# An expert-combine kernel on one core: a third tile loaded in two pieces from two queues, and a first tile made token by token

## The chip, the core and the metric

The kernel runs on one core of one Trainium2 chip. The metric is the device time of that core in microseconds (us), as the median of several executions. The profile is of one execution. It names engines by short names: DVE is VectorE, ACT is ScalarE, SP is SyncE, POOL is GpSimd. "ACTq" and "SPq" are the instruction sequencers of ScalarE and SyncE, which issue DMA transfers. TensorE is not used.

## The reference: what is computed

Each of 16 x 1024 = 16,384 tokens has the outputs of two experts, 512 fp32 values each, and two weights. The result is their weighted sum.

```python
# expert_outputs: (16, 1024, 2, 512) fp32   combine_weights: (16, 1024, 2) fp32
weights = combine_weights[..., np.newaxis]
return np.sum(expert_outputs * weights, axis=2)      # (16, 1024, 512) fp32
```

The profile counts 67.24 MB read and 33.55 MB written, with three floating-point operations for each value of the result. Nothing is used twice.

## The kernel before

The 16,384 tokens lie over 128 partitions, 128 tokens in each: 120 in ten tiles of 12 tokens, and 8 in a last, smaller tile. Below, the tiles are numbered 0 to 10. A token is 2 x 512 fp32 = 4 KB in a partition, so a tile of 12 tokens is 48 KB in a partition and 6 MB in all, and its result 24 KB and 3 MB.

```python
J, LAST = 12, 8                       # tokens of a tile, of the last tile
wpool = ...tile_pool(name="w", bufs=1)
ipool = ...tile_pool(name="in", bufs=4)          # four input tiles
wt = wpool.tile([P, per * k], dt)                # all weights
for t, c in ((0, main), (main, LAST)):           # weights: two loads, ScalarE's queue
    nc.scalar.dma_start(out=wt[...], in_=cw(t, c))
# ... a first activation on a constant ("warm") ...
for g in range(last + 1):                        # last = 10
    et = ipool.tile([P, J, k * h], dt)
    ot = ...                                     # the result lies in the first half of et
    for a, m in ((0, 2), (2, c - 2)) if g == 0 else ((0, c),):     # loads, SyncE's queue
        nc.sync.dma_start(out=et[:, a : a + m], in_=eo(t0 + a, m), ...)
    if g < last - 1:                             # tiles 0 to 8: all on VectorE
        nc.vector.tensor_tensor(out=ek, in0=ek, in1=wb, op=mult)              # L78
        nc.vector.tensor_tensor(out=ot, in0=et[:, :, 0:h],
                                in1=et[:, :, h : 2 * h], op=add)              # L79
        nc.scalar.dma_start(out=o(t0, c), in_=ot)                             # L80
        continue
    for i in range(c):                           # tiles 9 and 10: first half on ScalarE
        nc.scalar.activation(out=et[:, i, 0:h], in_=et[:, i, 0:h], func=copy,
                             scale=wt[:, 2 * t : 2 * t + 1])                  # L86
        if g == last:                            # tile 10: token by token
            nc.vector.scalar_tensor_tensor(out=ot[:, i, :], in0=et[:, i, h : 2 * h],
                scalar=wt[...], in1=et[:, i, 0:h], op0=mult, op1=add)         # L90
    if g < last:                                 # tile 9: second half in one go
        nc.vector.tensor_tensor(out=x1, in0=x1, in1=w1..., op=mult)           # L101
        nc.vector.tensor_tensor(out=ot, in0=et[:, :, 0:h], in1=x1, op=add)    # L102
    nc.sync.dma_start(out=o(t0, c), in_=ot[:, 0:c])                           # L103
```

The result is written over the tile's own input, so a load of tile g+4 can only be issued when the store of tile g has landed. The framework decides the order of instructions on each engine.

Of the kernel before, what the change touches and what calls it, by code (L numbers as in the profile page):

```python
# [1 line left out]

# [4 lines left out]


@with_exitstack
def kernel(  # L10
    ctx: ExitStack,
    tc: tile.TileContext,
    expert_outputs: bass.AP,
    combine_weights: bass.AP,
    out: bass.AP,
):

    nc = tc.nc  # L20
    b, s, k, h = expert_outputs.shape
    assert k == 2
    n = b * s
    P = nc.NUM_PARTITIONS
    per = n // P
    assert per * P == n
    J, LAST = 12, 8
    main = per - LAST
    assert main % J == 0
    eo = expert_outputs.rearrange("b s k h -> (b s) (k h)")  # L30
    cw = combine_weights.rearrange("b s k -> (b s) k")
    o = out.rearrange("b s h -> (b s) h")

    def rows(x):

        a = x[0 : P * main, :].rearrange("(p t) f -> p t f", p=P)
        b = x[P * main : n, :].rearrange("(p t) f -> p t f", p=P)
        return lambda t, c: a[:, t : t + c, :] if t < main else b[:, t - main : t - main + c, :]

    eo, cw, o = rows(eo), rows(cw), rows(o)  # L40

    dt = mybir.dt.float32
    mult = mybir.AluOpType.mult
    add = mybir.AluOpType.add
    copy = mybir.ActivationFunctionType.Copy

    last = main // J

    wpool = ctx.enter_context(tc.tile_pool(name="w", bufs=1))
    ipool = ctx.enter_context(tc.tile_pool(name="in", bufs=4))  # L50

    wt = wpool.tile([P, per * k], dt)

    for t, c in ((0, main), (main, LAST)):
        nc.scalar.dma_start(
            out=wt[:, k * t : k * (t + c)].rearrange("p (t k) -> p t k", k=k), in_=cw(t, c)
        )

    warm = wpool.tile([P, 1], dt)
    nc.scalar.activation(out=warm, in_=nc.const_aps.tensor(1.0, (P, 1), dt), func=copy)  # L60

    for g in range(last + 1):
        et = ipool.tile([P, J, k * h], dt)

        ot = et.rearrange("p j f -> p (j f)")[:, 0 : J * h].rearrange("p (j f) -> p j f", f=h)
        t0, c = g * J, J if g < last else LAST

        for a, m in ((0, 2), (2, c - 2)) if g == 0 else ((0, c),):
            nc.sync.dma_start(  # L69
                out=et[:, a : a + m],  # L70
                in_=eo(t0 + a, m),
                max_dma_last_dim=k * h * 4 if g + a == 0 else None,
            )
        if g < last - 1:

            wb = wt[:, g * J * k : (g + 1) * J * k].unsqueeze(2).to_broadcast([P, J * k, h])
            ek = et.rearrange("p j (k h) -> p (j k) h", k=k)
            nc.vector.tensor_tensor(out=ek, in0=ek, in1=wb, op=mult)  # L78
            nc.vector.tensor_tensor(out=ot, in0=et[:, :, 0:h], in1=et[:, :, h : 2 * h], op=add)  # L79
            nc.scalar.dma_start(out=o(t0, c), in_=ot)  # L80
            continue


        for i in range(c):
            t = t0 + i
            nc.scalar.activation(  # L86
                out=et[:, i, 0:h], in_=et[:, i, 0:h], func=copy, scale=wt[:, 2 * t : 2 * t + 1]
            )
            if g == last:
                nc.vector.scalar_tensor_tensor(  # L90
                    out=ot[:, i, :],
                    in0=et[:, i, h : 2 * h],
                    scalar=wt[:, 2 * t + 1 : 2 * t + 2],
                    in1=et[:, i, 0:h],
                    op0=mult,
                    op1=add,
                )
        if g < last:
            w1 = wt.rearrange("p (t k) -> p t k", k=k)[:, t0 : t0 + c, 1:2]
            x1 = et[:, :, h : 2 * h]  # L100
            nc.vector.tensor_tensor(out=x1, in0=x1, in1=w1.to_broadcast([P, c, h]), op=mult)  # L101
            nc.vector.tensor_tensor(out=ot, in0=et[:, :, 0:h], in1=x1, op=add)  # L102
        nc.sync.dma_start(out=o(t0, c), in_=ot[:, 0:c])  # L103


# [1 line left out]
_INS = ['expert_outputs', 'combine_weights']  # L107
_OUTS = [((16, 1024, 512), 'float32')]


# [23 lines left out]
```

## Time and profile before

| what | value |
|---|---|
| time, median of 3 (lowest to highest) | 238.96 us (238.95 to 240.68) |
| span of the profiled execution | 237.3 us |
| VectorE busy | 193.9 us, 82% |
| ScalarE busy | 14.0 us, 6% |
| DMA packets, bytes, mean rate | 3728, 100.80 MB, 425 GB/s |
| a 6 MB load, from issue to landing (median) | 29.9 us |
| a 3 MB store from ScalarE, from issue to landing (median) | 32.7 us |
| multiply of a tile (L78), sum of a tile (L79) | 12.955 us, 6.558 us |
| one token on ScalarE (L86), on VectorE (L90) | 0.707 us, 0.748 us |

The busy share of an engine over the whole span is an average. Here two rows of the page matter together: the row of VectorE and the row of the DMA engines, each with one digit for a fortieth of the span. The time from issue to landing of a transfer includes the time in which it waits behind others in its queue.

### The profile page before, as it was taken

The numbers are of one execution on the slowest core, as the hardware profiler recorded it, in microseconds if no ns is written. First come the engines' busy times: TensorE is split into PE (matmuls) and PEld (weight loads), VectorE is DVE, ScalarE is ACT, GpSimd is POOL, SyncE is SP. The second block draws the span as 40 slices with busy tenths as digits, with TensorE's granted clock in tenths as the row PEclk, the third lists the DMA queues.
The fourth block names the chain that finished last, engine by engine and source line by source line (L and its number), as shares of the span: only waits on it lengthen the run. The fifth ranks groups of instructions, "written<-read, shape, count | busy, mean of one in ns | idle before, by whom it ended". The sixth has DMA issues, their size and how long they took to land.

```text
span 237.3 us, 154 instructions
## 1 busy us (share of the span) xinstructions
DVE 193.9 (82%) x28; ACT 14.0 (6%) x22; POOL 0.2 (0%) x4
## 2 busy tenths in 40 slices
DVE  0008999999999999999999879969996998785710
ACT  2000000000000000000000000000000000740800
POOL 0000000000000000000000000000000000000000
DMA  8999999989899999999897999999997979999997
GB/s 308 443 456 406 398 431 497 398 356 505 356 439 435 427 464 464 398 398 522 348 522 344 452 427 435 464 464 398 398 522 340 530 336 460 458 403 442 402 438 309
DMA packets 3728, 100.80 MB, mean 425 GB/s; under 512 B 528, under 2 KB 656, under 8 KB 912
## 3 DMA queue, kind: packets, MB, share of 16 engines
q1 hardware_dynamic: 2144, 72.35, 71.1%
q10 hardware_dynamic: 1584, 28.44, 27.9%
HBM read 67.24 MB, written 33.55 MB: 425 GB/s over the span
## 4 chain that ended last, share of the span: by engine, by line
DMA 59%; DVE 33%; ACT 2%; DVEq 0%; ACTq 0%; issue 0%; SPq 0%
DMA et<-in_expert_outputs_dram 30%; DMA out_dram<-et 29%; DVE et L78 22%; DVE et L79 11%; ACT et L86 2%; DVE et L90 1%; DVEq L129 0%; ACTq L129 0%; SPq L69 0%; DVEq L78 0%; ACTq L86 0%
## 5 line engine op out<-in xcount | busy, mean ns | idle before, releaser
L78 DVE TENSOR_TENSOR et<-et,wt 128x12288 f32<-128x12288 f32 x9 | 116.6, 12955 | 25.2 <-DMA et<-in_expert_outputs_dram 25.2
L79 DVE TENSOR_TENSOR et<-et 128x6144 f32<-128x6144 f32 x9 | 59.0, 6558 | 0.3
L86 ACT ACTIVATE et<-et,wt 128x512 f32<-128x512 f32 x20 | 12.5, 707 | 209.2 <-DMA et<-in_expert_outputs_dram 209.2
L90 DVE SCALAR_TENSOR_TENSOR et<-et,wt 128x512 f32<-128x512 f32 x8 | 5.6, 748 | 3.9 <-ACT et L86 3.7
L101 DVE TENSOR_TENSOR et<-et,wt 128x6144 f32<-128x6144 f32 x1 | 6.6, 6559 | 2.3 <-DMA et<-in_expert_outputs_dram 2.3
L102 DVE TENSOR_TENSOR et<-et 128x6144 f32<-128x6144 f32 x1 | 6.6, 6559 | 0.9 <-ACT et L86 0.9
L60 ACT ACT_TABLE_LOAD x1 | 1.3, 1283 | 1.7 <-issue 1.7
L60 ACT ACTIVATE warm<-const-float32-1.0 128x1 f32<-128x1 f32 x1 | 0.2, 202 | 0.0
L118 POOL MEMSET const-bfloat16-1.0<- 128x1 bf16 x1 | 0.1, 102 | 0.0
L118 POOL MEMSET const-uint8-127<- 128x1 uint8 x1 | 0.1, 102 | 0.0
L118 POOL MEMSET const-float32-0.0<- 128x1 f32 x1 | 0.1, 99 | 0.2 <-issue 0.2
L118 POOL MEMSET const-float32-1.0<- 128x1 f32 x1 | 0.1, 99 | 0.0
## 6 DMA issues: line engine op xcount, KB each, us to landing
et<-in_expert_outputs_dram SPq DMA_DIRECT2D x9, 6144.0 KB, 29.9
out_dram<-et ACTq DMA_DIRECT2D x9, 3072.0 KB, 32.7
et<-in_expert_outputs_dram SPq DMA_DIRECT2D x1, 5120.0 KB, 17.3
et<-in_expert_outputs_dram SPq DMA_DIRECT2D x1, 4096.0 KB, 25.1
out_dram<-et SPq DMA_DIRECT2D x1, 3072.0 KB, 14.6
out_dram<-et SPq DMA_DIRECT2D x1, 2048.0 KB, 10.0
et<-in_expert_outputs_dram SPq DMA_DIRECT2D x1, 1024.0 KB, 5.4
wt<-in_combine_weights_dram ACTq DMA_DIRECT2D x1, 120.0 KB, 4.4
```

The source lines that it names most:

```text
L60: nc.scalar.activation(out=warm, in_=nc.const_aps.tensor(1.0, (P, 1), dt), func=copy)
L78: nc.vector.tensor_tensor(out=ek, in0=ek, in1=wb, op=mult)
L79: nc.vector.tensor_tensor(out=ot, in0=et[:, :, 0:h], in1=et[:, :, h : 2 * h], op=add)
L86: nc.scalar.activation(out=et[:, i, 0:h], in_=et[:, i, 0:h], func=copy, scale=wt[:, 2 * t : 2 * t + 1])
L90: nc.vector.scalar_tensor_tensor(out=ot[:, i, :], in0=et[:, i, h : 2 * h], scalar=wt[:, 2 * t + 1 : 2 * t + 2], in1=et[:, i, 0:h], op0=mul ...
L101: nc.vector.tensor_tensor(out=x1, in0=x1, in1=w1.to_broadcast([P, c, h]), op=mult)
L102: nc.vector.tensor_tensor(out=ot, in0=et[:, :, 0:h], in1=x1, op=add)
L118: nc = _bacc.Bacc("TRN2", target_bir_lowering=False, num_devices=1)
```

## The change

Tile 2 is loaded in two pieces, as tile 0 already was: ten tokens from SyncE's queue and the first two from ScalarE's, which has little to do between the weights and the first store. Tile 0 is no longer made with one multiply and one sum over the whole tile but token by token, as tile 10 is: ScalarE scales the first expert's half, VectorE multiplies the second by its weight and adds. It is for an earlier start of the arithmetic, since two tokens of tile 0 arrive ahead of the rest, and for an earlier first store. That store stays on ScalarE's queue.

```diff
-        for a, m in ((0, 2), (2, c - 2)) if g == 0 else ((0, c),):
-            nc.sync.dma_start(
+        for a, m in ((0, 2), (2, c - 2)) if g in (0, 2) else ((0, c),):
+            small = g in (0, 2) and a == 0
+            (nc.scalar if small and g == 2 else nc.sync).dma_start(
                 out=et[:, a : a + m],
                 in_=eo(t0 + a, m),
                 max_dma_last_dim=k * h * 4 if g + a == 0 else None,
             )
-        if g < last - 1:
+        if 0 < g < last - 1:
...
-            if g == last:
+            if g in (0, last):
                 nc.vector.scalar_tensor_tensor(
...
-        if g < last:
+        if 0 < g < last:
             w1 = ...
...
-        nc.sync.dma_start(out=o(t0, c), in_=ot[:, 0:c])
+        (nc.sync if g else nc.scalar).dma_start(out=o(t0, c), in_=ot[:, 0:c])
```

The order of instructions that the framework makes of it differs in more places than the diff. On ScalarE the load of the two tokens comes after the first two activations of tile 0. On VectorE the multiply of tile 9 comes ahead of the sum of tile 8, where before it came after. On ScalarE the store of tile 8 comes after all twelve activations of tile 9 and two of tile 10, where before it came after eight of tile 9.

## The prediction

> **What bounds the kernel now.** I read the slices of the page first, then the queue table, then stretches of the run, and only then the chain.
>
> From the page, the slices and the queues:
>
> ```profile
> DVE  0008999999999999999999879969996998785710
> ...
> DMA  8999999989899999999897999999997979999997
> ...
> q1 hardware_dynamic: 2144, 72.35, 71.1%
> q10 hardware_dynamic: 1584, 28.44, 27.9%
> HBM read 67.24 MB, written 33.55 MB: 425 GB/s over the span
> ```
>
> The two queues' packets fill 71.1% + 27.9% = 99.0% of 16 engines' time. VectorE is busy for 82% of the span and idles in holes after slice 24. q1 (SyncE: all loads, two stores) and q10 (ScalarE: weights, nine stores) share one set of engines, and that set has 1% to spare, some 2.4 us. The question is therefore only whether the engines run dry anywhere. Busy time by stretch (columns: us, VectorE, ScalarE, GpSimd, clock, DMA share, GB/s):
>
> ```profile
> 2.00:38.00 36.00, 19.33 (x2) 1.22 (x2) 0.00 (x0) 1.00 1.03 439
> 38.00:78.00 40.00, 39.93 (x6) 0.00 (x0) 0.00 (x0) 1.00 0.99 421
> ...
> 158.00:198.00 40.00, 36.35 (x4) 0.00 (x0) 0.00 (x0) 1.00 1.00 433
> 198.00:220.00 22.00, 15.79 (x3) 7.53 (x13) 0.00 (x0) 1.00 0.98 424
> 220.00:237.00 17.00, 5.57 (x8) 4.94 (x8) 0.00 (x0) 1.00 0.93 399
> ```
>
> One queue alone (2 to 38 us) moves 439 GB/s, two together 421 to 433: the rate doesn't depend on who asks. The last stretch is low only because the span ends inside it. So the end is fixed by 100.8 MB at about 433 GB/s, plus a start of about 2 us and any pause. The tail has none, and the timeline shows why:
>
> ```profile
> 194.12 6.56 DVE L79 TENSOR_TENSOR et<-et 128x6144 f32<-128x6144 f32 x1
> 202.96 0.72 ACT L86 ACTIVATE et<-et,wt 128x512 f32<-128x512 f32 x1 [199.73 <-DMA et<-in_expert_outputs_dram]
> 202.97 6.56 DVE L101 TENSOR_TENSOR et<-et,wt 128x6144 f32<-128x6144 f32 x1 [2.29 <-DMA et<-in_expert_outputs_dram]
> 203.26 0.34 ACTq L80 DMA_DIRECT2D out_dram<-et  x1
> ...
> 210.46 6.56 DVE L102 TENSOR_TENSOR et<-et 128x6144 f32<-128x6144 f32 x1 [0.93 <-ACT et L86]
> 217.04 9.79 SPq L103 DMA_DIRECT2D out_dram<-et  x2
> 219.93 5.01 ACT L86 ACTIVATE et<-et,wt 128x512 f32<-128x512 f32 x8 [9.51 <-DMA et<-in_expert_outputs_dram]
> ```
>
> Numbering tiles 0 to 10: the sum of tile 8 (L79 at 194.12) is done at 200.7, its store is issued at 203.26, and tile 9's store at 217.04. When the last load lands (219.85, by the chain) the engines still have parts of those two stores to write. They cover the last tile's arithmetic.
>
> **What the Trainium skill says.** "DMA: Bandwidth & Descriptors", section "Queues, rings and completion order": each engine serves its queues in turn, packet by packet. The trace agrees. Its packet records show a 48 KB load packet (1.815 us), then a 24 KB store packet (0.912 us), and so on; from 160 to 200 us the shares are 68.1% and 32.0%, and 1.815 to 0.912 is 66.6 to 33.4. The same page, "Issuing engines are not separate DMA queues": another issuing engine saves only issue time. The 439 GB/s with one queue agrees. "VectorE: DVE Perf Modes", section "The TRN2 errata": fp32 tensor_tensor takes (N+151)/0.96 ns, so 12,957 ns for 12,288 and 6,557 ns for 6,144; the profile has 12,955 and 6,558. Nothing moves there.
>
> **The change part by part.**
>
> *Bytes.* None added. Tile 2's 48 KB packet becomes 8 + 40 KB. By the trace's times (1.815 for 48 KB, 1.514 for 40, 0.912 for 24: 0.0376 us a KB and 0.01 us a packet), that is eight packets of 0.31 us in place of eight sixths of a longer one, under 0.1 us per engine. This is nothing.
>
> *First tile.* Removed from VectorE: 12.96 + 6.56 = 19.5 us. Added: 12 x 0.707 us on ScalarE (idle there) and 12 x 0.748 us on VectorE. The first two tokens start at about 6.2 (issue 0.73 + 5.4 to landing), the other ten at 18.5: 10 x 0.748 gives a first store at about 26.8 instead of 38.2. VectorE then waits for tile 1, so of 10.5 us saved little is passed on.
>
> *Two tokens on q10.* ScalarE issues them at about 6.3, right after its first two activations. They queue behind the 64-byte weight packets, which in the trace alternate with the 40 KB load packets and land at 1.2 + 17.1 = 18.3. So their eight packets alternate with tile 1's: tile 1 lands at 32.9 + 8 x 0.31 = 35.4 (32.9 is its issue at 1.8 plus 31.1), the two tokens at about the same time. Both are hidden.
>
> *First stores.* Store 0 is behind them in the ring and starts at about 35 instead of 43.3 (its first packet in the trace, 5 us after its issue). Beside tile 2's eight 40 KB packets it takes 8 x (1.514 + 0.912) = 19.4, to 54.3. Store 1 needs tile 1's 19.5 us of VectorE from 35.5: it is issued at 55.1, so ScalarE's ring is empty for a moment, and a fresh store starts some 5 us after issue (as store 0 did), at about 60. From there both rings are full.
>
> *When tile 9 lands.* It lands when q1 is through tile 9, delayed by each store packet slipped in before. Before: from 43.3 the loads had 2 + 7 x 8 packets to go, 66 turns with the completion descriptors, and with 8 data packets in 9 turns some 58.7 store packets. After: 8 of store 0, and about 59 turns from store 1 on, so 52.4: together 60.4. That is 1.7 x 0.912 = 1.6 us more; tile 9 lands at 204.5 instead of 202.9, at 205.3 if the pause is one packet shorter.
>
> *The tail.* This decides. The order of instructions on each engine (from the changed kernel's compiled program) differs at the end. VectorE has **tile 8's multiply, tile 9's multiply, tile 8's sum, tile 9's sum**; before, tile 8's sum came ahead of tile 9's multiply. ScalarE issues store 8 only after all twelve activations of tile 9 and two of tile 10, the first of which waits for the last load. So tile 8's sum, done before at 200.7, now waits for tile 9's landing and 6.56 us of multiply: it is ready at 204.5 to 205.3 + 13.1 = 217.6 to 218.4. The last load has nothing beside it once store 7 is out. Bytes say when: stores 8, 9 and 10 are 8 x (0.912 + 0.912 + 0.611) = 19.5 us, and the last packet of the trace ends at 236.2, so all before them is out at 216.7, whatever the order. Store 8 brings its first packet 1.2 us (the first load took 0.73 to 1.81) after 217.6 to 218.4, at 218.8 to 219.6. **The engines stand still for 2.1 to 2.9 us**, where before they never did. Tile 9's sum follows 6.5 us later, within store 8's 7.3, and the last tile's eight tokens (8 x 0.75) within store 9's, so no second pause.
>
> Sum: +0.1 for packets, +2.6 for the pause (a little above the middle, since I counted the gap between stores 0 and 1 long), nothing from the earlier start, which only shifts when bytes move. 238.96 + 2.7 = 241.7 us, +1.1%.
>
> **Rivals.** *Hidden anyway, about 239.0:* the engines never run dry because another store covers the end. The 99.0% speaks for it; the order of the two instruction lists against it. It needs tile 9 to land at 202 or earlier, and more stores ahead of it make it land later. *The pause is longer, 243 to 244:* if store 1 finds its ring not yet empty, the stores run without a gap, about 4 more packets slip in ahead of tile 9, it lands up to 3 us later, and each us is paid at the end. The margin is 55.1 against 54.3, so this is quite possible. *A gain, 237.5 to 238:* the earlier first store would have to raise the rate; with one queue already at 439 GB/s I see no room, and what idles at the start is about 2 us of issue and first packets, which the change does not touch.
>
> **Range and chances.** The pause can't be much under 1.3 us (tile 9 a packet or two early) nor much over 4.5 (no gap in the stores). With 0.5 us for the spread of the times (238.95 to 240.68 before) the range is 239.8 to 243.5. Over 2% faster (under 234.2) is below what 100.8 MB need: 0.01. Over 2% slower (above 243.7) needs the longest pause: 0.09. Within 2%: 0.90.
>
> **What would show it.** In the changed profile: first store issued near 27; tile 1's multiply near 35.5; store 1 near 55; on VectorE a hole after tile 8's multiply until tile 9 lands near 205; store 8 issued near 218, store 9 near 224.5; a stretch of 2 to 3 us near 217 to 219 with no DMA. It is wrong if the DMA row shows no hole in the tail, if tile 8's sum runs before tile 9 lands, or if the rate between 60 and 200 us is not 433 GB/s.

## The result, and the profile after

The changed kernel takes 243.03 us (median of 6, 242.79 to 243.5) against 239.01 us, a ratio of 1.0155 with a 95% interval of 1.0129 to 1.018 (the two medians alone give 1.0168). It is slower by about 4 us, inside the range predicted and 1.3 us above the predicted time.

From the page of the changed kernel, the slices of VectorE and of the DMA engines and the two queues:

```profile
DVE  0207308999999998899699969969996970899930
...
DMA  8999999999999999999999999999999999986997
...
q1 hardware_dynamic: 2144, 71.30, 69.0%
q10 hardware_dynamic: 1728, 29.49, 28.6%
```

The engines' packets now fill 97.6% of the span instead of 99.0%, and the DMA row has an 8 and a 6 in slices 36 and 37 (a slice is 6 us, so these are 211 to 223 us). VectorE works less (76% of the span), and its new holes are at the start, where the DMA row stays at 8 and 9. The tail in stretches, the changed kernel first (columns: us, VectorE, ScalarE, GpSimd, clock, DMA share, GB/s):

```profile
198.00:217.00 19.00, 10.92 (x2) 7.46 (x12) 0.00 (x0) 1.00 0.95 410
217.00:220.00 3.00, 3.00 (x2) 1.81 (x3) 0.00 (x0) 1.00 0.10 41
220.00:241.00 21.00, 11.05 (x9) 3.31 (x6) 0.00 (x0) 1.00 0.92 394
```

and the kernel before in the same 3 us:

```profile
217.00:220.00 3.00, 0.01 (x1) 0.07 (x1) 0.00 (x0) 1.00 0.96 412
```

From 217.1 to 220.0 us all sixteen engines stand still. The trace records start, length, size and queue of every packet. Summed over the engines, the idle time here is 3.15 us for each; the kernel before had no such pause, and both lose some 2 us at the start. The timeline of the changed kernel, the start and the tail:

```profile
6.24 0.34 ACTq L70 DMA_DIRECT2D et<-in_expert_outputs_dram  x1
...
26.14 0.35 ACTq L104 DMA_DIRECT2D out_dram<-et  x1
36.94 12.96 DVE L79 TENSOR_TENSOR et<-et,wt 128x12288 f32<-128x12288 f32 x1 [10.83 <-DMA et<-in_expert_outputs_dram]
...
184.24 12.96 DVE L79 TENSOR_TENSOR et<-et,wt 128x12288 f32<-128x12288 f32 x1 [2.23 <-DMA et<-in_expert_outputs_dram]
206.07 7.46 ACT L87 ACTIVATE et<-et,wt 128x512 f32<-128x512 f32 x12 [181.20 <-DMA et<-in_expert_outputs_dram]
206.08 6.56 DVE L102 TENSOR_TENSOR et<-et,wt 128x6144 f32<-128x6144 f32 x1 [8.88 <-DMA et<-in_expert_outputs_dram]
212.55 6.55 DVE L80 TENSOR_TENSOR et<-et 128x6144 f32<-128x6144 f32 x1
217.54 1.33 ACT L87 ACTIVATE et<-et,wt 128x512 f32<-128x512 f32 x2 [4.01 <-DMA et<-in_expert_outputs_dram]
219.02 6.55 DVE L103 TENSOR_TENSOR et<-et 128x6144 f32<-128x6144 f32 x1
219.14 0.34 ACTq L81 DMA_DIRECT2D out_dram<-et  x1
```

Tile 8's multiply ends at 197.2, then VectorE waits 8.88 us for tile 9, multiplies it, and only then makes tile 8's sum (L80 at 212.55). That store is issued at 219.14 instead of 203.26, when the last load has already landed (217.5, where ScalarE's two activations begin). Nothing was left for the engines to move in between.

### The profile page after: what moved, and what is told of

It reads as the page before. It is cut to its first block, busy times and chain, and to the rows that moved or that the text cites. A ratio compares the mean times of both kernels' runs of the same rounds, so it can differ in the third digit from the quotient of the medians.

```text
span 241.1 us, 185 instructions
## 1 busy us (share of the span) xinstructions
DVE 182.6 (76%) x38; ACT 21.6 (9%) x34; POOL 0.2 (0%) x4
## 4 chain that ended last, share of the span: by engine, by line
DMA 65%; DVE 28%; issue 2%; DVEq 1%; SPq 0%
DMA et<-in_expert_outputs_dram 41%; DMA out_dram<-et 24%; DVE et L79 16%; DVE et L80 8%; DVE et L103 3%; DVE et L91 2%; DVEq L130 0%; SPq L70 0%; DVEq L91 0%; DVEq L79 0%
## 5 line engine op out<-in xcount | busy, mean ns | idle before, releaser
L79 DVE TENSOR_TENSOR et<-et,wt 128x12288 f32<-128x12288 f32 x8 | 103.7, 12957 | 21.4 <-DMA et<-in_expert_outputs_dram 21.4
L80 DVE TENSOR_TENSOR et<-et 128x6144 f32<-128x6144 f32 x8 | 52.5, 6557 | 0.2
L87 ACT ACTIVATE et<-et,wt 128x512 f32<-128x512 f32 x32 | 20.1, 709 | 199.9 <-DMA et<-in_expert_outputs_dram 199.3
L91 DVE SCALAR_TENSOR_TENSOR et<-et,wt 128x512 f32<-128x512 f32 x20 | 13.8, 747 | 18.1 <-ACT et L87 17.8
L103 DVE TENSOR_TENSOR et<-et 128x6144 f32<-128x6144 f32 x1 | 6.6, 6552 | 0.0
```

## The experiments

The theory was: a pause of the DMA engines in the tail makes the loss, and it comes of two things together, tile 8's sum standing behind tile 9's multiply, and tile 9 landing later. Rival A was that the earlier stores at the start cost the time by themselves; rival B that ScalarE's order holds store 8. Every kernel below computes the whole result.

### Tile 8's sum put back ahead of tile 9's multiply

```diff
 # changed kernel; behind(x, y): x is issued after y on its engine, without a wait
-            nc.vector.tensor_tensor(out=x1, in0=x1, in1=..., op=mult)
+            mul9 = nc.vector.tensor_tensor(out=x1, in0=x1, in1=..., op=mult)
+            behind(mul9, add8)
```

> The changed kernel, with one order on VectorE put back: tile 8's sum ahead of tile 9's multiply (on ScalarE the framework then sets store 8 ahead of tile 10's activations by itself). Theory (the tail's order makes the pause): tile 9 still lands at about 206, store 8 is issued near 206 instead of 219, no stretch without DMA, 239.1 to 239.5 us. Rival A (the earlier stores at the start cost the time, since tile 9 lands 3 us later): 242 to 243. Rival B (store 8 is late because it stands behind tile 10's activations on ScalarE): this run can't tell it from the theory; the next two do.

Measured: 239.82 us (239.75 to 240.13), 1.0035 of the kernel before (1.0022 to 1.0048). Its timeline:

```profile
197.36 6.56 DVE L85 TENSOR_TENSOR et<-et 128x6144 f32<-128x6144 f32 x1
...
206.21 6.56 DVE L107 TENSOR_TENSOR et<-et,wt 128x6144 f32<-128x6144 f32 x1 [2.29 <-DMA et<-in_expert_outputs_dram]
206.62 0.34 ACTq L86 DMA_DIRECT2D out_dram<-et  x1
```

Tile 9 lands as late as in the changed kernel (206.2), but the sum fits into the wait for it, store 8 goes at 206.6 and there is no pause. Of 4.0 us, 3.2 come back with this one order (store 8's place on ScalarE followed from it). Rival A falls as the main cause, but 0.8 us stay without any pause, more than I expected; they are taken up below.

### Store 8 alone held back

```diff
 # the kernel of the experiment before
+            if g == last and i == 1:
+                behind(store8, act)        # store 8 after two activations of tile 10
```

> As the run before, but store 8 is put back behind two of tile 10's activations on ScalarE, so it waits for the last load although tile 8's sum is ready near 205. Theory (both orders delay store 8, and the later of the two counts): the last load lands alone near 217.3, store 8 is issued near 217.5 and its first packet goes at about 218.4; the pause is about 1.5 us instead of 3.1, 240.6 to 241.4 us. Rival A: 242 to 243. Rival B: the same as the changed kernel, 243.

Measured: 242.19 us (242.05 to 242.29), 1.0132 (1.0117 to 1.0147), a miss by 0.8 us. The timeline tells why:

```profile
217.72 0.34 ACTq L86 DMA_DIRECT2D out_dram<-et  x1
...
218.35 0.75 DVE L98 SCALAR_TENSOR_TENSOR et<-et,wt 128x512 f32<-128x512 f32 x1 [5.64 <-ACT et L92]
219.01 6.55 DVE L111 TENSOR_TENSOR et<-et 128x6144 f32<-128x6144 f32 x1
```

Store 8 is issued at 217.72, as expected, for a pause of 1.75 us. But the framework set one token of tile 10 ahead of tile 9's sum (L98 ahead of L111), so that sum waited too, and its store left a second pause of 0.57 us near 226. Together 2.32 us; the time is 2.37 us above the experiment before. So ScalarE's order can hold store 8 as well, though in the changed kernel it isn't what ends last, as the next run shows.

### Store 8 freed from ScalarE

```diff
 # changed kernel
-            nc.scalar.dma_start(out=o(t0, c), in_=ot)
+            (nc.scalar if g < last - 2 else nc.sync).dma_start(out=o(t0, c), in_=ot)
```

> The changed kernel with store 8 issued from SyncE's queue behind the last load, so that no activation of ScalarE stands ahead of it; VectorE's order stays (tile 9's multiply ahead of tile 8's sum). Theory: store 8 still waits for tile 8's sum near 219.1, nothing gained, 242.7 to 243.3 us. Rival B (ScalarE's order is the cause): store 8 goes earlier, 239 to 241.

Measured: 243.02 us (242.81 to 243.07), the changed kernel's time.

```profile
212.90 6.55 DVE L80 TENSOR_TENSOR et<-et 128x6144 f32<-128x6144 f32 x1
...
219.47 0.35 SPq L81 DMA_DIRECT2D out_dram<-et  x1
```

With no activation ahead of it, store 8 still goes only when tile 8's sum is done. Rival B falls.

### The late tail on the kernel before

```diff
 # kernel before
+            behind(add8, mul9)             # tile 8's sum after tile 9's multiply
+            if g == last and i == 1:
+                behind(store8, act)
```

> The kernel before, with the changed kernel's tail order forced on it: on VectorE tile 8's sum behind tile 9's multiply, on ScalarE store 8 behind two of tile 10's activations. Nothing of the change's start is in it. Theory: tile 9 lands at 202.9 as before, tile 8's sum is ready at 202.9 + 13.1 = 216.0, the last load lands alone near 217.3 and frees store 8 near 217.5; pause about 1.5 us, 240.4 to 241.0 us, so about 40% of the loss without the change's start. Rival A: 239.0.

Measured: 240.78 us (240.58 to 240.82), 1.0074 (1.0057 to 1.009), as expected. The pause is 1.59 us:

```profile
209.26 6.55 DVE L84 TENSOR_TENSOR et<-et 128x6144 f32<-128x6144 f32 x1
...
216.96 0.72 ACT L91 ACTIVATE et<-et,wt 128x512 f32<-128x512 f32 x1 [6.72 <-DMA et<-in_expert_outputs_dram]
217.09 0.34 ACTq L85 DMA_DIRECT2D out_dram<-et  x1
```

Here tile 8's sum is ready at 215.8, and store 8 waits for the last load on ScalarE: the roles are changed about.

### The late sum alone on the kernel before

```diff
 # kernel before
+            behind(add8, mul9)
-            nc.scalar.dma_start(out=o(t0, c), in_=ot)
+            (nc.scalar if g < last - 2 else nc.sync).dma_start(out=o(t0, c), in_=ot)
```

> The kernel before with VectorE's late order alone: tile 8's sum behind tile 9's multiply, and store 8 on SyncE's queue behind the last load, so that ScalarE's order plays no part. Theory (the pause is the late sum against the end of the last load): tile 9 lands at 202.9, the sum is ready at 216.0, just before the last load's packets end near 216.7; store 8's first packet comes 0.9 us after its issue, so a pause of 0.2 to 0.4 us: 239.1 to 239.5 us. With the changed kernel's start the same order costs 4 us, because tile 9 lands 3.1 us later. If the order alone costs the same with any start: 242 to 243.

Measured: 239.5 us, 1.0017 (0.9997 to 1.0037). Thirteen of 15 executions took 239.4 to 239.7, the other two 241.40 and 241.85. There are two profiles, the first of an execution of 241.40 us, the second of one of 239.39 us.

> A second profile of the kernel before with VectorE's late order and store 8 on SyncE's queue. In the profile of the first, an execution of 241.40 us against a median of 239.5, tile 9 landed at 204.8 and the engines stood still for 2.2 us. Theory: in an execution of about 239.5 tile 9 lands near 202.9, tile 8's sum is ready near 216.0, and the pause is 0.3 to 0.6 us. If the pause is as long at 239.5 as at 241.4, the pause isn't what the order costs.

The tail of the first profile:

```profile
204.83 6.56 DVE L106 TENSOR_TENSOR et<-et,wt 128x6144 f32<-128x6144 f32 x1 [8.88 <-DMA et<-in_expert_outputs_dram]
...
217.88 0.35 SPq L85 DMA_DIRECT2D out_dram<-et  x1
```

and of the second:

```profile
202.83 6.56 DVE L106 TENSOR_TENSOR et<-et,wt 128x6144 f32<-128x6144 f32 x1 [8.86 <-DMA et<-in_expert_outputs_dram]
...
215.89 0.35 SPq L85 DMA_DIRECT2D out_dram<-et  x1
```

Tile 9 lands 2.0 us later in the first, the store is issued 2.0 us later, the pause is 2.22 us against 0.37, and the time 2.01 us longer. It is the same program both times; what differs is when tile 9 lands, and the rest follows. With tile 9 at 202.8 VectorE's late order costs 0.4 us by the medians (the interval above doesn't exclude zero), at 206.1, in the changed kernel, 3.2: the pause needs both. Where ScalarE's order is late too, as in the run before this one, it costs 1.7 us even with tile 9 at 202.8.

### Each half of the change alone

The first tile token by token, tile 2 in one piece:

```diff
 # changed kernel
-        for a, m in ((0, 2), (2, c - 2)) if g in (0, 2) else ((0, c),):
+        for a, m in ((0, 2), (2, c - 2)) if g == 0 else ((0, c),):
```

> One half of the change alone: the first tile token by token, tile 2 loaded in one piece. The framework keeps the tail's order as in the kernel before (tile 8's sum ahead of tile 9's multiply, store 8 ahead of tile 10's activations). Theory: first store near 26, tile 9 lands later than 202.9 (the early store slips in ahead of loads), yet no pause at the end: 238.9 to 239.4 us. Rival A (early stores cost): 240.5 or more.

Measured: 240.34 us (240.25 to 240.62), 1.0047 (1.0029 to 1.0065), about 1 us above what I expected, and nearer to rival A's 240.5.

```profile
198.80 6.56 DVE L79 TENSOR_TENSOR et<-et 128x6144 f32<-128x6144 f32 x1
...
207.65 6.56 DVE L101 TENSOR_TENSOR et<-et,wt 128x6144 f32<-128x6144 f32 x1 [2.29 <-DMA et<-in_expert_outputs_dram]
207.91 0.34 ACTq L80 DMA_DIRECT2D out_dram<-et  x1
```

No pause: tile 9 lands at 207.6, later than in any other kernel here, and store 8 is issued at 207.9, since tile 8's sum came first. But two of the sixteen engines end 1.0 us after most others, at 237.2. By the packet records the engines wait 0.8 us more for the last of them than in the kernel before, most of the 1.04 us by which this profile's span is longer. So the early stores do cost something without a pause, and rival A is right about that part.

Tile 2 in two pieces, the first tile whole:

```diff
 # kernel before
-        for a, m in ((0, 2), (2, c - 2)) if g == 0 else ((0, c),):
-            nc.sync.dma_start(
+        for a, m in ((0, 2), (2, c - 2)) if g in (0, 2) else ((0, c),):
+            (nc.scalar if g == 2 and a == 0 else nc.sync).dma_start(
```

> The other half alone: tile 2 in two pieces, two tokens from ScalarE's queue, the first tile whole as before. The framework now orders tile 8's multiply ahead of tile 7's sum, and stores 7 and 8 behind two activations of tile 9. Theory (only a pause of the DMA engines costs): stores 7 and 8 come late, near 203, the loads fill the engines meanwhile and land earlier, and four stores are left for the end, so no pause: 238.9 to 239.5 us. Rival A (the split itself costs, by delaying tile 1 by 2.5 us): 240 or more.

Measured: 239.6 us (239.38 to 239.95), 1.0015 (1.0006 to 1.0024). The order moved again:

```profile
182.50 12.96 DVE L78 TENSOR_TENSOR et<-et,wt 128x12288 f32<-128x12288 f32 x1 [8.81 <-DMA et<-in_expert_outputs_dram]
...
201.96 0.34 ACTq L80 DMA_DIRECT2D out_dram<-et  x1
```

VectorE waits 8.81 us for tile 8 before it makes tile 7's sum, the same fault one tile earlier, and store 7 goes at 202 instead of 179. It makes no pause there: loads still fill the engines. So the half changes are 1.25 and 0.5 us slower than the kernel before, and neither has the 4 us.

### The first tile in one transfer

```diff
 # kernel before
-        for a, m in ((0, 2), (2, c - 2)) if g == 0 else ((0, c),):
+        for a, m in ((0, c),):
...
-                max_dma_last_dim=k * h * 4 if g + a == 0 else None,
```

> The kernel before with the first tile loaded in one transfer of 6 MB, in 48 KB packets, instead of 1 MB in 4 KB packets and 5 MB. The only idle time of the engines is the start, so this is where a gain could lie. Theory (bytes and packets set the time): 24 packets per engine (16 of 4 KB, 8 of 40 KB) become 8, at 0.01 us each, and the first packets' slow start of about 0.7 us may be shorter: 238.2 to 238.9 us. If the start doesn't matter: 239.0.

Measured: 239.94 us (238.95 to 240.53), 1.0017 (1.0000 to 1.0034). No gain. The first 48 KB packets take 2.4 to 3.0 us instead of 1.815, so the slow start isn't paid per packet, and in the profiled execution one engine ends 0.8 us after the next. Four of the 14 executions took 239.0 to 239.1, as the kernel before does; the other ten, the profiled one among them, 239.8 to 240.5. None of the kernels tried beats the one before.

## Why the prediction was right

*The bound* held: outside the start, the pauses and an uneven end the engines are never idle, in every kernel profiled. The rate held too, with 432, 433 and 440 GB/s in the three stretches of 40 us from 78 to 198 us. With the same start, the time follows the pause; the start itself adds up to 1.25 us without one.

| kernel | tile 9 lands, us | pause, us | time, us |
|---|---|---|---|
| before | 202.9 | 0 | 239.0 |
| before, late sum alone (second profile) | 202.8 | 0.37 | 239.4 |
| before, late sum alone (first profile) | 204.8 | 2.22 | 241.4 |
| before, late tail | 202.8 | 1.59 | 240.8 |
| tile 2 in two pieces alone | 200.8 | 0 | 239.6 |
| first tile token by token alone | 207.6 | 0 | 240.3 |
| first tile in one transfer | 204.7 | 0 | 239.9 |
| changed, tile 8's sum first | 206.2 | 0 | 239.8 |
| the same, store 8 late | 206.1 | 1.75 + 0.57 | 242.2 |
| changed, store 8 on SyncE | 206.4 | 3.18 | 243.0 |
| changed | 206.1 | 3.15 | 243.0 |

*First tile and first stores*: as predicted. The two tokens were issued at 6.24, store 0 at 26.14 (26.8), store 1 at 56.5 (55.1), with its first packet at 59.9 (60). Tile 1 landed at 36.9, not 35.4.

*When tile 9 lands*: 206.1, where the turns gave 204.5 to 205.3. This is the term that was mis-sized. The packet records give the number that I had reckoned: 62.1 store packets per engine end before tile 9 has landed, not 60.4, against 59.0 in the kernel before (58.7 reckoned). That is 3.1 x 0.912 = 2.85 us of the 3.1 us by which tile 9 lands later; the stretched packets described at the end give another 0.2. The gap between stores 0 and 1 was three load packets, the shorter of the two I had counted, which explains about one of the missing packets; why there was nearly one more is not shown.

*The tail*: the order decided it, as put. Store 8 was issued at 219.14 (217.6 to 218.4), late by what tile 9 was late; its first packet came 0.85 us after, not 1.2. The pause is 3.15 us, not 2.1 to 2.9.

*The sum* left out a second term. Without a pause the changed kernel is still 0.8 us slower than before. I had 0.1 for packets and nothing for the earlier start, and "nothing" was wrong. In the profile with tile 8's sum first the span is 0.71 us longer than before: the packets take 0.24 us more an engine, the engines wait 0.23 us more for the last one at the end, and the time from the last packet to the end of the span is 0.23 us longer (1.35 against 1.12). No run removes one of these parts alone, so their causes are open. In the changed kernel's own profile, 3.75 us longer than before, the pause is 3.15 us, the packets 0.41 and the time after the last packet 0.23; the start adds 0.1, and the even end takes 0.16 off.

That the range held is in part luck. The missing term and the longer pause both went the same way, and the upper end of the range had been set for another case, stores 0 and 1 without a gap.

*Rivals*: "hidden anyway" is what happens when tile 8's sum comes first. "The pause is longer" was the nearer one in size, but not by its cause: store 1 did find its ring (ScalarE's queue on each engine) empty: the last packet of store 0 ended at 55.0, and store 1 was issued at 56.5. No kernel tried was faster than the one before.

## What to carry to other kernels

Where the DMA engines are full, ask first where they run dry, and look at the end: in these runs a late store made no pause while loads were left to move (store 7 by 23 us, with tile 2 in two pieces), and once there were none, each us of delay was about a us of pause. An edit at the start of a program can change the order of instructions at its end, so compare the whole order on each engine and not the diff alone. Where an order is what matters, pin it: here one pin on VectorE took 3.2 of the 4.0 us away.

## What the runs showed of the hardware

Two things were new to me. The first store of a kernel comes with a delay on each DMA engine: by the packet records, a load packet just ahead of the first store packets is stretched, in the kernel before at 41 us from 1.815 to 2.2 to 2.4 us on all sixteen. The stretch moves with the first store: on most engines it begins at 28 us with the tokens alone (first store packet at 30.6), at 33 in the changed kernel (34.9) and at 41 in the kernel before (43.3). The two tokens that the changed kernel loads on the same queue from 17.5 us on show next to none until then (0.03 us an engine up to 30 us). Summed from 24 to 60 us it is 0.6 to 0.7 us an engine in the six profiles with tile 2 in one piece, and in the five with tile 2 in two pieces 0.8 (changed kernel), 0.9, 0.9, 1.1 and 1.3 (store 8 on SyncE). It is part of the 0.8 us that stays without a pause; no run took it away.

And the engines don't stay in step: the slowest sets each landing and the end. In the first profile of the late sum alone, tile 9's last data packets end at 201.3 us on the median engine and at 203.45 on the slowest; in the second, at 201.3 and 201.5. That is why tile 9 landed 2.0 us apart in the same program. In the kernels without a pause the engines end within 0.45 (before), 0.6 and 0.8 us of each other, with the tokens alone within 1.2 us (two engines late; the records have 2.3 us of stretched packets in all between 60 and 82 us, which fits) and with the first tile in one transfer within 1.3. After a pause it is 0.14 to 0.18 us: in the changed kernel all sixteen start store 8 within 0.15 us.
